# Transposed input kept for two blocks, a shorter ring of second-level operands, and stores issued by GpSimd, in a two-level Strassen-Winograd MLP kernel

## The chip, the cores and the metric

The kernel runs on one core of one Trainium2 chip. The metric is the device time in microseconds. Three runs of the kernel before took 933.02, 934.6 and 937.8 us; their median is 934.6 us. One more run was profiled.

## The reference

A batch of 16 x 512 = 8192 rows goes through two matrix products with a bias and a GELU between them:

```python
batch, m, k, h, n = 16, 512, 768, 3072, 768
y = np.matmul(x, w1) + b1
y = 0.5 * y * (1.0 + erf(y / np.sqrt(2.0)))
return np.matmul(y, w2).astype(np.float32)
```

All arrays are float32; the kernel computes its products in fp16 operands and adds in float32.

## The kernel before

The 8192 rows are taken in eight blocks of 1024 rows, numbered 0 to 7 (`sb` in the code). Each block goes through a first product (x with w1, then bias and GELU) and a second product (with w2).

Both products use Strassen's method in Winograd's form: a product of 2 x 2 blocks is made of seven smaller products of sums and differences of the blocks instead of eight. The seven are done in the order p1, p7, p5, p3, p6, p4, p2, each accumulated in a PSUM bank (`bX`, `bY`, `bW`, `bZ`), with copies and additions by ScalarE and VectorE between them.

- **First product** (`Unit1`, matmuls at L333): 12 units per block, one for each pair of 128 columns of the hidden layer. One of the seven products is three matmuls of 128 x 512; it takes 0.65 us. The weights of a unit, a tile `wt` of seven slots (672 KB), sit in a pool of four buffers. From block 2 on they are read from a scratch array `w1s` in DRAM, where block 1 has written them with their sums and differences (`load_wt`, L157; `keep`, L174). Unit k loads the weights of unit k + 3 in its slot 5.
- **Second product, blocks 0 and 1** (`Unit2`, L371): four units of seven products of twelve matmuls of 128 x 384; one product takes 1.95 us. Its operands lie in the array `w2o` in SBUF. The two halves of the output row block are kept in `osb`, of which there is one, and stored by SyncE (L385, L390). Beside it, `split_w2` makes the second-level operands of w2 in 28 steps: a subtraction by VectorE into a staging buffer (`stage`), then one or two writes of 288 KB to the scratch array `w2s` by SyncE (L206).
- **Second product, blocks 2 to 7** (`Unit3`, L422): a second level of the same method. Seven units of seven products of twelve matmuls of 128 x 192; one product takes 0.99 us. Each of the 49 products reads one second-level operand, 288 KB, which SyncE loads from `w2s` into a ring of 15 buffers (`load_ring`, L239): the load for product n + 15 is issued when product n is done. Results collect in four float32 arrays `par`; two additions by GpSimd (L467) finish one of them, and eight stores of 384 KB per block are issued by SyncE (L446).

x is loaded 128 rows at a time by GpSimd, with a cast to fp16, into one of three buffers `xh` (`load_x`, L248), and transposed by a DMA that SyncE issues (`transpose_dma`, L255) into `XT`. Block 0 alone transposes with TensorE. VectorE then makes four sums of the quarters of `XT` (`x_sums`); one of them is written over a quarter of `XT`. There is one `XT`: the eight loads and eight transposes for the next block are issued during the second product, once the last unit of the first product has read it.

The order of all work is written out by hand. `period(i, j, fill)` interleaves the seven products of unit i with the rest of unit j before it, and calls `fill` at six slots; `fill_mm1`, `fill_mm2_one` and `fill_mm2_two` issue there what belongs to the slots: loads, transposes, VectorE sums from the lists `soon`, `queue` and `slow`. Every engine works through its own queue in order: a DMA that waits holds all that stands behind it in SyncE's or GpSimd's queue.

Everything but the weights and x shares one SBUF array, `arena`, cut by hand. The staging buffers and the sums `GS` of blocks 0 and 1 lie over parts that blocks 2 to 7 use otherwise, and the first product's `tmps` lie over `par[0]` and `par[3]`.

## Time and profile before

| | |
|---|---|
| median of three runs | 934.6 us |
| the profiled execution's own time | 931.55 us |
| its span on the core | 929.7 us |
| TensorE busy | 869.7 us, 94% |
| VectorE busy | 665.6 us, 72% |
| ScalarE busy | 417.1 us, 45% |
| GpSimd busy | 116.4 us, 13% |
| DMA, mean over the span | 240 GB/s |
| granted TensorE clock, mean | 0.977 |

In the profile PE is TensorE, DVE is VectorE, ACT is ScalarE, POOL is GpSimd, and SPq is SyncE's DMA issue. A timeline row gives start in us, duration in us, engine, line and operation, out<-in, shape and count, and in brackets the idle time before it with its releaser. A row of waits gives the total in us, how often, and the longest. A row of a table of windows gives the window, its length, the busy time (and count of instructions) of PE, PE's weight loads, DVE, ACT and POOL, the granted clock, the DMA engines' busy share and GB/s. A row of DMA issues ends with KB and the us from issue to landing. Numbers after tile names are buffers (`bX_143`, `w1s_72`).

Block 2's first product runs from about 260 to 311 us of the span, its second to about 361. The blocks after it begin their first products at about 366, 478, 590, 704 and 815 us; block 7's second product ends the span.

### The profile page before, as it was taken

How to read it: one execution, taken by the hardware profiler on the slowest of the kernel's cores; microseconds unless marked ns; L12 is line 12 of the kernel's file. 1: busy time of each engine (PE TensorE's matmuls, PEld its weight loads, DVE VectorE, ACT ScalarE, POOL GpSimd, SP SyncE). 2: the span in 40 equal slices, each digit the busy share in tenths (PEclk: the TensorE clock that was granted, in tenths of full speed). 3: DMA queues.
4: the chain of work that ended last, by engine and by line, in shares of the span. 5: the costliest groups of instructions: out<-in, count | busy, mean ns of one | idle time of the engine just before them, and what ended most of it. 6: DMA issues, size and time to landing. Idle time of an engine off the chain costs nothing.

```text
span 929.7 us, 16276 instructions
## 1 busy us (share of the span) xinstructions
PE 869.7 (94%) x6276; PEld 565.6 (61%) x6276; DVE 665.6 (72%) x1151; ACT 417.1 (45%) x680; POOL 116.4 (13%) x146
## 2 busy tenths in 40 slices
PE   5999999997999997999989999799997999899997
PEld 2434654444544796447964499544994459854697
DVE  3688666663546896479965799467994679945997
ACT  2655117740167521774217732377213772157610
POOL 5552102300100012000210002000030000200002
PEclk7999999999999998999999999999998999999999
DMA  9998999959848599685997689965998749978485
GB/s 156 111 187 112 259 339 227 244 192 302 186 146 281 156 266 347 235 285 139 296 348 256 215 201 300 353 234 178 248 282 313 250 165 271 317 262 280 162 286 205
DMA packets 184206, 222.97 MB, mean 240 GB/s; under 512 B 106944, under 2 KB 127424, under 8 KB 184128
## 3 DMA queue, kind: packets, MB, share of 16 engines
q1 hardware_dynamic: 124736, 195.18, 65.1%
q0 software_dynamic: 59392, 26.75, 23.0%
q8 instruction: 49, 0.80, 0.3%
q14 instruction: 29, 0.24, 0.1%
HBM read 189.74 MB, written 47.87 MB: 256 GB/s over the span
## 4 chain that ended last, share of the span: by engine, by line
PE 66%; DMA 15%; DVE 12%; ACT 2%; issue 2%; POOL 1%; SPq 1%; DVEq 0%; ACTq 0%; POOLq 0%
PE bY_144 L333 9%; PE bY_145 L333 8%; PE bX_143 L333 6%; DVE arena L127 6%; PE bW L333 5%; PE bX_142 L333 5%; PE bZ L333 5%; DMA wt<-in_w_dram 4%; DMA wt<-w1s_72 4%; PE bY_145 L422 4%; PE bY_144 L422 4%; PE bW L422 3%; PE bZ L422 3%; PE bX_142 L422 2%; PE bX_143 L422 2%
## 5 line engine op out<-in xcount | busy, mean ns | idle before, releaser
L333 PEld LDWEIGHTS <-wt 128*128 128x128 f16 x2016 | 197.7, 99 | 271.4 <-DMA wt<-w1s_72 22.9
L422 PEld LDWEIGHTS <-arena 128*128 128x128 f16 x2664 | 226.0, 99 | 21.1 <-issue 16.6
L348 ACT ACTIVATE G_134<-arena,b1t 128x1024 f16<-128x1024 f32 x96 | 110.3, 1149 | 63.8 <-DVE arena L505 63.8
L127 DVE TENSOR_TENSOR arena<-arena 128x1536 f16<-128x1536 f16 (+5 forms) x176 | 127.7, 746 | 0.9
L492 ACT COPY pw<-bW 128x512 f32<-128x512 f32 (+1 forms) x146 | 80.9, 554 | 93.8 <-PE bW L422 44.3
L248 POOL DMA_DIRECT2D xh<-in_x_dram x56 | 29.9, 536 | 598.2 <-DMA XT<-xh 591.5
L482 DVE TENSOR_TENSOR arena<-bY_145,pw 128x512 f32<-128x512 f32 (+1 forms) x52 | 35.4, 681 | 94.9 <-PE bY_145 L333 69.0
L333 PE MATMUL bX_143<-XT,wt 128*128 128x512 f16 x288 | 80.1, 388 | 13.1 <-DMA wt<-w1s_72 12.9
L333 PE MATMUL bX_142<-XT,wt 128*128 128x512 f16 x288 | 80.5, 389 | 8.8 <-DMA wt<-w1s_72 8.8
L505 DVE TENSOR_TENSOR arena<-bZ,pw 128x512 f32<-128x512 f32 (+1 forms) x104 | 70.5, 678 | 19.6 <-PE bZ L333 13.8
L333 PE MATMUL bW<-XS_136,wt 128*128 128x512 f16 x288 | 80.4, 389 | 4.0 <-DVE wt L127 4.0
L333 PE MATMUL bY_144<-XT,wt 128*128 128x512 f16 x288 | 78.0, 379 | 3.5 <-DVE bZ L520 3.4
L482 DVE TENSOR_TENSOR arena<-bY_144,pw 128x512 f32<-128x512 f32 (+1 forms) x52 | 35.4, 681 | 63.1 <-PE bY_144 L333 35.8
L333 PE MATMUL bY_145<-XT,wt 128*128 128x512 f16 x288 | 77.8, 379 | 2.1 <-DVE bZ L520 1.2
L333 PE MATMUL bZ<-XS_138,wt 128*128 128x512 f16 x288 | 77.8, 379 | 0.0
L475 ACT COPY bY_145<-bX_143 128x512 f32<-128x512 f32 (+1 forms) x73 | 39.9, 547 | 83.3 <-DVE arena L454 39.5
L475 ACT COPY bY_144<-bX_142 128x512 f32<-128x512 f32 (+1 forms) x73 | 40.4, 554 | 69.8 <-DVE arena L454 39.6
L422 PE MATMUL bY_144<-arena 128*128 128x192 f16 x612 | 61.7, 253 | 5.4 <-DVE bZ L515 5.4
L422 PE MATMUL bY_145<-arena 128*128 128x192 f16 x612 | 60.5, 250 | 5.4 <-DVE bZ L515 5.4
L371 PEld LDWEIGHTS <-arena 128*128 128x128 f16 x384 | 38.0, 99 | 32.3 <-issue 7.0
L127 DVE TENSOR_TENSOR arena<-arena,G_133 128x1024 f16<-128x1024 f16 (+4 forms) x86 | 48.5, 564 | 1.8
L161 POOL DMA_DIRECT2D wt<-in_w_dram x48 | 39.5, 831 | 79.8 <-DVE wt L127 35.3
(87 smaller groups left out, 1178.5 us busy)
## 6 DMA issues: line engine op xcount, KB each, us to landing
out_dram<-arena SPq DMA_DIRECT2D x64, 384.0 KB, 6.3
xh<-in_x_dram POOLq DMA_DIRECT2D x56, 192.0 KB, 6.6
wt<-in_w_dram POOLq DMA_DIRECT2D x48, 192.0 KB, 7.3
arena<-in_w_dram POOLq DMA_DIRECT2D x16, 288.0 KB, 9.0
wt<-w1s_72 SPq DMA_DIRECT2D x6, 672.0 KB, 9.1
wt<-w1s_78 SPq DMA_DIRECT2D x6, 672.0 KB, 10.3
wt<-w1s_73 SPq DMA_DIRECT2D x6, 672.0 KB, 8.8
wt<-w1s_79 SPq DMA_DIRECT2D x6, 672.0 KB, 5.1
```

The lines of the kernel that those rows point to most:

```text
L127: nc.vector.tensor_tensor(out=o, in0=a, in1=b, op=op)
L161: nc.gpsimd.dma_start(out=wt[:, 2 * half:2 * half + 2, :, :].rearrange("p a k c -> p (a k) c"), in_=w1r[:, :, c0:c0 + P])
L248: nc.gpsimd.dma_start(out=xh, in_=xr[:, sb * 8 + t, :])
L333: nc.tensor.matmul(out=dst[:, 0:RH], lhsT=self.wt[:, slot, c, :], rhs=a[:, c, :], start=first and c == 0, stop=c == self.C - 1, skip_group ...
L348: nc.scalar.activation(out=G2[:, hi, :, :], in_=self.tmp, func=GELU, bias=b1t[:, NH + hi:NH + hi + 1])
L371: nc.tensor.matmul(out=dst[:, 0:N2], lhsT=a, rhs=w2o[:, slot, :, c, :], start=first and c == 0, stop=c == self.C - 1, skip_group_check=True)
L422: nc.tensor.matmul(out=dst[:, t * N4:(t + 1) * N4], lhsT=a, rhs=w[:, c, :], start=first and c == 0 and t == 0, stop=c == NQ - 1, skip_grou ...
L475: nc.scalar.copy(out=bY[u.g % 2][:, 0:u.F], in_=bX[u.g % 2][:, 0:u.F])
L482: nc.vector.tensor_tensor(out=u.c22(), in0=bY[u.g % 2][:, 0:u.F], in1=w[:, 0:u.F], op=ADD)
L492: nc.scalar.copy(out=w[:, 0:u.F], in_=bW[:, 0:u.F])
L505: nc.vector.tensor_tensor(out=u.c12(), in0=bZ[:, 0:u.F], in1=w[:, 0:u.F], op=ADD)
```

## The change

Four things change together.

- There are two arrays `XT`, used in turn by even and odd blocks. In blocks 2 to 6 the eight x loads and eight transposes of the next block are issued in the first product (units 1 to 8 and 3 to 10, slot 3) instead of the second. The sums of x stay in the last unit of the second product. Block 0's and block 1's stay where they were.
- The ring has 10 buffers instead of 15, which frees the space for the second `XT`. It is filled in units 3 to 7 of the first product. `stage` has four buffers instead of five, in `par[0]` and `par[3]`, and `GS` moves too. Since `tmps` lie there, the three steps of `split_w2` in block 1's first product are gone; 12 of the 28 steps run in block 0's second product (before: 15) and 16 in block 1's (before: 10).
- The weights for units 0, 1 and 2 of the next block are loaded in units 0, 5 and 6 of the second product (slot 6), before in units 4, 5 and 6.
- The eight stores per block at L446 are issued by GpSimd, not by SyncE.

```diff
-    XT = wp.tile([P, 2, 2 * KQ, RH], F16, name="XT")
+    XTs = [wp.tile([P, 2, 2 * KQ, RH], F16, name=f"XT{k}") for k in range(2)]
...
-    RING = 15
+    RING = 10
...
-    stage = [cut(o, WB, "p (c n) -> p c n", c=NQ)
-             for o in (*range(14 * NH * N4, o_par - 4 * NH * P - WB + 1, WB),
-                       o_par + 2 * PAR, o_par + 2 * PAR + WB)]
+    stage = [cut(o_par + k * PAR + d * WB, WB, "p (c n) -> p c n", c=NQ)
+             for k in (0, 3) for d in range(2)]
...
-    GS = [cut(o_par - (4 - k) * NH * P, NH * P, "p (c r) -> p c r", c=NH) for k in range(4)]
+    GS = [cut(o + k * NH * P, NH * P, "p (c r) -> p c r", c=NH)
+          for o in (14 * NH * N4, o_par + 2 * PAR) for k in range(2)]
...
-        def transpose_dma(t):
-            nc.sync.dma_start_transpose(out=xT_of(t), in_=xhs[t])
+        def transpose_dma(sb, t):
+            nc.sync.dma_start_transpose(out=xT_of(sb, t), in_=xhs[t])
...
             def store(self, r):
...
-                nc.sync.dma_start(out=orr[:, s0:s0 + 2, right * N2:(right + 1) * N2],
+                nc.gpsimd.dma_start(out=orr[:, s0:s0 + 2, right * N2:(right + 1) * N2],
...
         def fill_mm1(sb, k, slot):
...
-            if sb == 1 and slot == 2 and k % 4 == 2:
-                slow.pop(0)[1]()
+            if slot == 3 and sb >= ONE and sb + 1 < nsb:
+                if 1 <= k < 9:
+                    load_x(sb + 1, k - 1)
+                if 3 <= k < 11:
+                    transpose_dma(sb + 1, k - 3)
...
         def fill_mm2_one(sb, k, slot):
...
-            if slow and slot > 1 and (k > 0 or sb > 0):
+            if slot > 1 and len(slow) > (16, 0)[sb]:
                 slow.pop(0)[1]()
...
         def fill_mm2_two(sb, k, slot):
...
             if sb + 1 < nsb:
-                if k == 0 and slot == 1:
-                    load_next_x(sb + 1, range(3))
-                if k == 1 and slot == 4:
-                    for t in range(3):
-                        transpose_dma(t)
-                    load_next_x(sb + 1, range(3, 6))
-                if k == 3 and slot == 1:
-                    for t in range(3, 6):
-                        transpose_dma(t)
-                    load_next_x(sb + 1, range(6, 8))
-                if k in (4, 5, 6) and slot == 6:
-                    load_wt((sb + 1) * NH + k - 4)
-                if k == 4 and slot == 4:
-                    for t in range(6, 8):
-                        transpose_dma(t)
+                if k in (0, 5, 6) and slot == 6:
+                    load_wt((sb + 1) * NH + max(k - 4, 0))
                 if k == 6 and slot == 1:
                     prep_wt((sb + 1) * NH)
-                    x_sums(queue)
+                    x_sums(sb + 1, queue)
```

How the queues change is seen at three places. The first is SyncE's queue at the end of block 2's second product. L255 is a transpose of x, L239 a ring load, L446 a store, L157 a load of first-product weights (`w1s_72` and `w1s_78` are those of units 0 and 1). Before:

```order
L255 DMA_TRANSPOSE XT<-xh 128x6x128 x2
L239 DMA arena<-w2s_99 128x1152
L446 DMA out_dram<-arena 128x2x384 x2
L239 DMA arena<-w2s_104 128x1152
L157 DMA wt<-w1s_72 128x2688
L239 DMA arena<-w2s_100 128x1152
L239 DMA arena<-w2s_101 128x1152
L446 DMA out_dram<-arena 128x2x384 x2
L157 DMA wt<-w1s_78 128x2688
L446 DMA out_dram<-arena 128x2x384 x2
L157 DMA wt<-w1s_73 128x2688
```

With the change, at the same place:

```order
L239 DMA arena<-w2s_99 128x1152
L239 DMA arena<-w2s_104 128x1152
L239 DMA arena<-w2s_100 128x1152
L239 DMA arena<-w2s_101 128x1152
L157 DMA wt<-w1s_78 128x2688
L157 DMA wt<-w1s_73 128x2688
L157 DMA wt<-w1s_79 128x2688
```

Transposes and stores have left, and the load of `w1s_72` has moved 35 rows ahead, to the fifth row of the second product. The second place is SyncE's queue in units 4 to 6 of block 2's first product, with the change:

```order
L157 DMA wt<-w1s_81 128x2688
L239 DMA arena<-w2s_88 128x1152
L239 DMA arena<-w2s_89 128x1152
L255 DMA_TRANSPOSE XT_136<-xh 128x6x128
L157 DMA wt<-w1s_76 128x2688
L239 DMA arena<-w2s_119 128x1152
L239 DMA arena<-w2s_90 128x1152
L255 DMA_TRANSPOSE XT_136<-xh 128x6x128
```

Before, the same rows stand there without the two transposes. The third place is SyncE's queue in block 1's second product, from the transposes of its third unit on (L206 is a write of a second-level operand, L386 and L391 are the output stores, which stood at L385 and L390). With the change:

```order
L255 DMA_TRANSPOSE XT_135<-xh 128x6x128 x3
L206 DMA w2s_131<-arena 128x1152
L206 DMA w2s_128<-arena 128x1152
L206 DMA w2s_129<-arena 128x1152
L386 DMA out_dram<-arena 128x768
L206 DMA w2s_111<-arena 128x1152
L206 DMA w2s_105<-arena 128x1152
L391 DMA out_dram<-arena 128x768
L206 DMA w2s_109<-arena 128x1152
L206 DMA w2s_106<-arena 128x1152
L255 DMA_TRANSPOSE XT_135<-xh 128x6x128 x2
```

Before, no write of a second-level operand was left here: the three transposes were followed by the two output stores and the two transposes.

42 lines of the change are left out of this document (21 added, 21 removed).

## The prediction

> **What bounds the kernel now.** I read part 1 of the page first, then TensorE's waits, then the timeline around them.
>
> ```profile
> span 929.7 us, 16276 instructions
> PE 869.7 (94%) x6276; PEld 565.6 (61%) x6276; DVE 665.6 (72%) x1151; ACT 417.1 (45%) x680; POOL 116.4 (13%) x146
> ```
>
> ```profile
> PE bX_143 L333 <- DMA wt<-w1s_72: 12.9, 3, 5.3
> PE bX_142 L333 <- DMA wt<-w1s_72: 8.8, 2, 5.9
> ```
>
> TensorE is busy for 94%, so only its 60 us of idle time, and what follows each idle stretch, can be won. The largest wait (in total us, times, longest) is 12.9 + 8.8 = 21.7 us in five places: the first weights of a block, at the five turns from the second product of blocks 2 to 6 into the next block's first product. Every other row of that view is smaller. The timeline of TensorE shows each turn: the product before the wait, the wait, and the first product after which the pace is again one per 0.65 us (L333) or 0.99 us (L422).
>
> ```profile
> 359.98 1.15 PE L422 MATMUL bX_142<-arena 128*128 128x192 f16 x12
> 366.40 1.46 PE L333 MATMUL bX_143<-XT,wt 128*128 128x512 f16 x3 [5.27 <-DMA wt<-w1s_72]
> 373.73 0.81 PE L333 MATMUL bX_143<-XT,wt 128*128 128x512 f16 x3
> ...
> 473.77 1.15 PE L422 MATMUL bX_143<-arena 128*128 128x192 f16 x12
> 477.84 1.46 PE L333 MATMUL bX_142<-XT,wt 128*128 128x512 f16 x3 [2.91 <-DMA wt<-w1s_72]
> 484.08 0.81 PE L333 MATMUL bX_142<-XT,wt 128*128 128x512 f16 x3
> ...
> 583.97 1.15 PE L422 MATMUL bX_142<-arena 128*128 128x192 f16 x12
> 596.54 0.81 PE L333 MATMUL bX_143<-XT,wt 128*128 128x512 f16 x3
> ...
> 696.57 1.15 PE L422 MATMUL bX_143<-arena 128*128 128x192 f16 x12
> 711.31 0.81 PE L333 MATMUL bX_142<-XT,wt 128*128 128x512 f16 x3
> ...
> 810.87 1.15 PE L422 MATMUL bX_142<-arena 128*128 128x192 f16 x12
> 814.65 1.08 PE L333 MATMUL bX_143<-XT,wt 128*128 128x512 f16 x3 [2.63 <-DMA wt<-w1s_72]
> 821.24 0.81 PE L333 MATMUL bX_143<-XT,wt 128*128 128x512 f16 x3
> ```
>
> Between the first and last row of each turn stand four products of the second kind and three of the first: 4 x 0.99 + 3 x 0.65 = 5.9 us of work. The elapsed times are 13.75, 10.31, 12.57, 14.74 and 10.37 us; the losses are 7.8, 4.4, 6.7, 8.8 and 4.5, together **32.2 us**. So a turn costs half as much again as its wait. The rest is the clock, here in the stretch right after the shortest of the waits (the last three columns are granted clock, DMA share, GB/s):
>
> ```profile
> 814.65:818.00 3.35, 3.35 (x17) 2.45 (x18) 0.31 (x1) 0.57 (x1) 0.00 (x0) 0.57 1.04 409
> ```
>
> The clock is at 0.57 for some 3 us even after a wait of 2.63 us. The Trainium skill ("TensorE: Matmul & The Clock Gate", Part 1) puts the drop to half rate after an idle window of about 3.4 us; by that rule the two turns with waits of 2.91 and 2.63 us would lose only these, and the sum below would be smaller by (4.4 - 2.9) + (4.5 - 2.6) = 3.4 us. The row decides against it here.
>
> **Why the weights are late.** SyncE's timeline before the first turn:
>
> ```profile
> 335.20 7.53 SPq L255 DMA_TRANSPOSE XT<-xh  x3
> ...
> 354.29 1.41 SPq L446 DMA_DIRECT2D out_dram<-arena  x2
> ...
> 356.34 0.47 SPq L157 DMA_DIRECT2D wt<-w1s_72  x1
> ```
>
> SyncE issues in order. The weight load goes out at 356.34, behind eight transposes (three of them in the first row) and the stores, and lands at 366.4, 10 us later, since the DMA engines are full (second row below; the columns are as above):
>
> ```profile
> 260.00:311.00 51.00, 51.00 (x239) 23.20 (x238) 31.90 (x54) 38.71 (x61) 0.00 (x0) 1.00 0.60 207
> 311.00:365.00 54.00, 48.21 (x562) 46.31 (x560) 50.48 (x85) 12.94 (x25) 9.09 (x10) 1.00 1.00 264
> ...
> 872.00:925.00 53.00, 51.09 (x597) 49.23 (x596) 49.13 (x85) 12.46 (x25) 4.79 (x2) 1.00 0.73 235
> ```
>
> These are block 2's first and second product and block 7's second. Block 7 has no successor, so no x and no transposes: that is the second product as the change leaves it.
>
> **The change part by part.** *First weights (L157), transposes and x moved out of the second product.* The program issues the load in unit 0 instead of unit 4 of seven units of 7 us, some 40 us before its use. The sums of x stay in unit 6:
>
> ```profile
> 358.48 0.96 DVE L127 TENSOR_TENSOR XS_136<-XT 128x1536 f16<-128x1536 f16 x1 [0.20 <-DMA XT<-xh]
> ...
> 362.49 0.95 DVE L127 TENSOR_TENSOR XS_138<-XT,XS_137 128x1536 f16<-128x1536 f16 x1
> ```
>
> With no wait, the new block's first product would start at 361.0, the one that reads XS_136 at 362.6 (0.65 + 0.99 later) and the one that reads XS_138 at about 368.5; the sums ended at 359.4 and 363.4, so 3 us of cover stay. Gain: 32.2 us if nothing else is late there.
>
> *Ring of 10.* A load is issued when the product ten ahead has been read, so it has 9 products, 9 x 0.99 = 8.9 us. Block 7's second product has nothing but ring loads and stores about; its slowest ring load:
>
> ```profile
> arena<-w2s_93 SPq DMA_DIRECT2D x1, 288.0 KB, 4.8
> ```
>
> (us from issue to landing): 4 us of cover. Cost 0. In block 2's full stretch the slowest early one took longer than the 8.9 us, and there each late load would cost TensorE some 0.4 us, more where a clock drop follows:
>
> ```profile
> arena<-w2s_92 SPq DMA_DIRECT2D x1, 288.0 KB, 9.3
> ```
>
> *x and transposes in the first product.* Here is the price. Its weights and ring loads now:
>
> ```profile
> 378.46 0.34 SPq L157 DMA_DIRECT2D wt<-w1s_74  x1
> ```
>
> ```profile
> 387.98 0.81 PE L333 MATMUL bX_143<-XT,wt 128*128 128x512 f16 x3
> ```
>
> ```profile
> wt<-w1s_74 SPq DMA_DIRECT2D x1, 672.0 KB, 3.8
> ```
>
> ```profile
> DMA packets 3452, 10.35 MB, mean 211 GB/s; under 512 B 384, under 2 KB 384, under 8 KB 3448
> ```
>
> A unit takes 7 products x 0.65 = 4.53 us. The weights issued at 378.46 are read at 387.98, 9.5 us later, and land after 3.8: slack 5.7 us. The last row is block 2's first product (262 to 311): 10.35 MB in about 30 us of DMA time (0.60 x 49 to 51) is 345 GB/s, so 2.0 us for a weight tile, 0.85 for a ring load: 3.7 us per unit with two ring loads. What an x load and a transpose cost together no row isolates. Base: the two second products differ by 54 x 1.00 - 53 x 0.73 = 15.3 us; block 2's has two weight tiles more (4.0) and two stores less (2 x 1.14 us at 345 GB/s), so 13.6 us for eight pairs, **1.7 us** each. Upper end: three transposes held SyncE for 7.53 us, 2.5 each, and 384 KB of x at 345 GB/s take 1.1: 3.6 us. In units 3 to 7 pairs and ring loads coincide. Base: 3.7 + 1.7 = 5.4 us per unit, 0.9 over, 4.4 us behind after five units, inside the slack: no stall. Upper end: 7.3, 2.8 over, 13.9 behind, 8.2 us of stall per block, 41 us over blocks 2 to 6. Below nothing it cannot go. I take 0.6 us per block, **3 us**, near the base, because that comes from whole stretches while SyncE's 7.53 us also holds queueing behind ring loads.
>
> *Stores from GpSimd.* They leave SyncE's order; GpSimd has only two additions per block beside them, and the buffers they free are wanted tens of us later. Only the last store is on the path, after the last addition:
>
> ```profile
> 925.44 0.56 DVE L454 TENSOR_TENSOR arena<-bY_145,arena 128x384 f32<-128x384 f32 x1 [0.43 <-PE bY_145 L422]
> ```
>
> ```profile
> 343.93 0.53 POOL L248 DMA_DIRECT2D xh<-in_x_dram  x1 [13.37 <-DMA XT<-xh]
> ```
>
> From the addition's end to the span's end are 3.7 us. GpSimd's issue of one x load (128 rows) takes 0.53 us against SyncE's 0.34 for a weight load; a store has 256 rows. Plus 0.2 us if only the issue differs, up to 3 us if the landing nearly doubles: I take **1 us**.
>
> *Blocks 0 and 1.* w2's split keeps 16 of its 28 steps for block 1's second product (10 before) and has none in block 1's first product. Now:
>
> ```profile
> 135.15 2.12 PE L371 MATMUL bZ<-arena 128*128 128x384 f16 x12 [0.48 <-DVE arena L127]
> ...
> 191.09 0.81 PE L333 MATMUL bY_144<-XT,wt 128*128 128x512 f16 x3 [1.56 <-DVE bZ L520]
> ...
> 224.29 2.11 PE L371 MATMUL bZ<-arena 128*128 128x384 f16 x12
> 231.50 3.73 PE L371 MATMUL bY_144<-arena 128*128 128x384 f16 x12 [5.09 <-ACT bY_144 L475]
> 235.06 2.11 PE L371 MATMUL bY_145<-arena,G_134 128*128 128x384 f16 x12
> ```
>
> ```profile
> 189.66 0.32 SPq L206 DMA_DIRECT2D w2s_123<-arena  x1
> ```
>
> The wait of 1.56 us on VectorE's copy ended 1.4 us after the write of a split step was issued, in a queue of additions that VectorE works through in order; I count it as gone. The other stall, 235.06 - 224.29 less two products of 1.95, 6.9 us, is an output store stuck behind transposes, weights and writes of w2; all of these stay, with one write more in front (0.85 us), and units 2 and 3 get transposes and writes together, as block 0 has them, where the first row (0.48 us) is the only wait. Plus 1.5, bounds 0 and another 6.9. Net **0**.
>
> *Sum:* -32.2 + 3 + 1 + 0 = -28.2 us; the span goes from 929.7 to 901.5. The profiled run's own time is 931.55, 1.85 over its span, and the median of the runs shown, 934.6, is 3 us above that: **906 us**.
>
> **The rivals.** *Half given back:* a pair costs 2.5 us, between the bounds: 6.2 per unit, 1.7 over, 8.4 behind, 2.7 of stall per block, 13 us; 934.6 - 32.2 + 13 + 1 = 916. For it: a transpose alone is at 2.5 in the 7.53 us row. Against: the 15.3 us difference.
>
> *The wait moves, no gain:* at the turn the second-level operands or the sums of x arrive late instead, as the ring is a third shorter. For it: the 9.3 us above. Against: block 7's 4.8 at most. A loss like the present one gives 932.
>
> *Slower, the first product becomes the DMA's:* the weights of units 6 to 11 come late, in each of five blocks, with a clock drop behind each. Price at the upper end: -32.2 + 41 + 1 = +10, 944. It decides from 6.5 us of stall per block, which is a pair at 3.3 us. Against: block 2's first product has 0.60 of DMA time used; eight pairs at 1.7 add 13.6 us and take five ring loads (4.3 us) away, 40 of 51 us. The Trainium skill ("DMA: Bandwidth & Descriptors", Issuing engines are not separate DMA queues) says that all issuers share the same 16 engines; by it GpSimd's x is no cheaper than SyncE's would be, which is how this rival counts it.
>
> **How the numbers follow.** Forecast 0.66 (900 to 911), half given back 0.16 (911 to 926), no gain 0.07, slower 0.11. Range 898 to 926: the low end is the whole 32.2 gained with the runs' own spread of 3 us, the high end the second case's. The likeliest case's own range is 900 to 911. A change of 0.5% (4.7 us) is about what can be told from none: faster 0.82, same 0.07, slower 0.11.
>
> **What would show it.** Right: the five waits on w1s_72 gone, no clock under 0.95 around the turns; DMA share near 0.75 in second and 0.85 in first products; weights landing after 4 to 9 us in units 3 to 8; ring loads under 6 us. Wrong: L333 waiting for weights or L422 for ring loads late in a product; a landing of weights above 9.5 us; block 1 losing more than one store's wait.

## The result, and the profile after

The changed kernel takes 906.86 us (median of four runs, 906.44 to 908.34), the kernel before, in four runs beside it, 933.81 us. The ratio is 0.9711 with a 95% interval of 0.9673 to 0.9748: 27 us, or 2.9%, faster. The prediction said 906. Its sum came out, but several of its terms did not, and one edit was priced without its main effect, as the experiments show; that the errors nearly cancel is luck.

The head of the page after, to be read against the first two rows of the prediction (the profiled execution's own time is 908.34 us):

```profile
span 906.2 us, 16269 instructions
PE 860.2 (95%) x6276; PEld 560.6 (62%) x6276; DVE 666.9 (74%) x1151; ACT 417.5 (46%) x680; POOL 148.1 (16%) x194
```

TensorE's busy time fell by 9.5 us although it executes the same 6276 matmuls: the stretches at a lowered clock at the turns are gone, which is likely most of it. GpSimd's rose by 32 us; it now issues 48 stores.

TensorE's waits after (total us, times, longest). Lines past the first sixty or so stand one lower than before: L333 is now L334, L422 is L423, L515 is L516; in experiments whose edit adds lines they move by one or a few more.

```profile
PE bY L423 <- DVE bZ L516: 13.3, 12, 1.8
...
PE bX L334 <- DMA wt<-w1s: 1.5, 3, 0.8
```

The 21.7 us of waits on the first weights are gone; of all waits on loads from `w1s` 1.5 us are left, in three places inside first products. The largest wait is now one that the prediction did not name: VectorE's addition that writes `bZ` (L516; the last expectation below calls it a copy), 13.3 us where the two rows of before give 5.4 + 5.4 = 10.8.

The first turn in TensorE's timeline, which answers to the prediction's first pair of rows:

```profile
363.03 1.15 PE L423 MATMUL bX<-arena 128*128 128x192 f16 x12
364.02 0.81 PE L334 MATMUL bX<-XT,wt 128*128 128x512 f16 x3
364.67 1.15 PE L423 MATMUL bY<-arena 128*128 128x192 f16 x12
...
368.94 1.46 PE L334 MATMUL bX<-XT,wt 128*128 128x512 f16 x6
```

From the first row to the last are 5.91 us, exactly the work of four products of 0.99 and three of 0.65 us; before it was 13.75. The other four turns take 5.9 us as well.

The granted clock and the DMA share by stage, with the columns of before (the last three are clock, DMA share and GB/s): block 2's first product, its second, and block 3's first product.

```profile
262.00:313.00 51.00, 49.91 (x231) 22.07 (x229) 31.23 (x53) 37.96 (x60) 2.64 (x5) 1.00 0.87 225
313.00:367.00 54.00, 51.66 (x592) 48.94 (x591) 51.76 (x87) 14.60 (x28) 8.61 (x8) 1.00 0.87 291
...
366.00:413.00 47.00, 46.95 (x234) 22.30 (x232) 28.27 (x47) 34.72 (x55) 6.12 (x11) 1.00 1.04 271
```

The clock is at 1.00 throughout. The DMA share fell in the second product, to 0.87 where the prediction expected some 0.75, and rose in the first further than the 0.85 expected: 0.87 in block 2, and 1.04 in the part of block 3's that the last row covers. Yet TensorE hardly waits for it, because the loads have room. The loads issued in block 3's first product (366 to 413 us; the last number is the median from issue to landing):

```profile
wt<-w1s SPq DMA_DIRECT2D x8, 672.0 KB, 6.3
arena<-w2s SPq DMA_DIRECT2D x10, 288.0 KB, 7.6
```

Weights land after 6.3 us in the middle, inside the 9.5 that they have. The slowest of these eight takes 10.0 us and the slowest in block 2 10.1; the 1.5 us of waits lie in these two blocks.

**Where the time went, by stretches.** One profile of a kernel cannot be compared with one of another over the whole span: block 1's first product differs by up to 5 us between profiles of kernels whose code there is the same (shown below). So I cut the span at three places of TensorE's timeline: the first L334 of block 1, the first L372 of block 1's second product, and the first L334 of block 2 (131.25, 196.71 and 253.66 us in the profile after).

| profile | block 1, first product | block 1, second | block 2 to the end |
|---|---|---|---|
| before | 64.4 | 56.9 | 677.1 |
| after | 65.5 | 57.0 | 652.5 |
| after, second profile | 60.4 | 57.9 | 652.7 |

From block 2 on the change gains 24.5 us, and two profiles of it agree within 0.2 us. The parts: the five turns -32.2; the longer of a block's two waits for the addition into `bZ` grows from 1.33 to 1.75 us in each of six blocks, +2.5; the end after the last addition grows from 3.7 to 7.3 us, +3.6; block 2's first product takes 59.9 instead of 58.3 us, +1.6. Their sum is -24.5. (In the second profile block 2's first product takes 58.6 us, and about as much is lost in later first products instead.)

### The profile page after: what moved, and what is told of

It reads as the page before. It is cut to its first block, busy times and chain, and to the rows that moved or that the text cites. A ratio compares the mean times of both kernels' runs of the same rounds, so it can differ in the third digit from the quotient of the medians.

```text
span 906.2 us, 16269 instructions
## 1 busy us (share of the span) xinstructions
PE 860.2 (95%) x6276; PEld 560.6 (62%) x6276; DVE 666.9 (74%) x1151; ACT 417.5 (46%) x680; POOL 148.1 (16%) x194
## 4 chain that ended last, share of the span: by engine, by line
PE 67%; DVE 14%; DMA 10%; issue 4%; POOL 2%; ACT 2%; SPq 0%; POOLq 0%; DVEq 0%; ACTq 0%
PE bY L334 17%; PE bX L334 11%; PE bY L423 8%; DVE arena L127 7%; PE bW L334 5%; PE bZ L334 5%; PE bY L372 5%; PE bX L423 5%; DMA wt<-in_w_dram 4%; DMA wt<-w1s 4%; PE bX L372 3%; PE bW L423 3%; PE bZ L423 3%; DMA out_dram<-arena 1%; PE bZ L372 1%
## 5 line engine op out<-in xcount | busy, mean ns | idle before, releaser
L334 PEld LDWEIGHTS <-wt 128*128 128x128 f16 x2016 | 197.1, 98 | 250.9 <-issue 19.6
L423 PEld LDWEIGHTS <-arena 128*128 128x128 f16 x2664 | 221.2, 98 | 20.8 <-issue 15.1
L483 DVE TENSOR_TENSOR arena<-bY,pw 128x512 f32<-128x512 f32 (+1 forms) x104 | 70.8, 680 | 153.9 <-PE bY L334 98.7
L334 PE MATMUL bY<-XT,wt 128*128 128x512 f16 x576 | 155.8, 379 | 7.5 <-DVE bZ L521 7.3
L334 PE MATMUL bX<-XT,wt 128*128 128x512 f16 x576 | 143.0, 381 | 1.6 <-DMA wt<-w1s 1.5
L476 ACT COPY bY<-bX 128x512 f32<-128x512 f32 (+1 forms) x146 | 80.4, 551 | 131.9 <-DVE arena L455 105.0
L349 ACT ACTIVATE G<-arena,b1t 128x1024 f16<-128x1024 f32 x96 | 110.3, 1149 | 64.3 <-DVE arena L506 64.3
L423 PE MATMUL bY<-arena 128*128 128x192 f16 x1224 | 115.6, 246 | 13.3 <-DVE bZ L516 13.3
L334 PE MATMUL bW<-XS,wt 128*128 128x512 f16 x288 | 78.7, 383 | 4.0 <-DVE wt L127 4.0
L334 PE MATMUL bY<-XS,wt 128*128 128x512 f16 x288 | 79.1, 384 | 1.0 <-DVE wt L127 0.4
L334 PE MATMUL bZ<-XS,wt 128*128 128x512 f16 x288 | 78.5, 382 | 0.0
L423 PEld LDWEIGHTS <-G 128*128 128x128 f16 x864 | 72.5, 98 | 4.8 <-issue 1.9
L372 PEld LDWEIGHTS <-arena 128*128 128x128 f16 x384 | 38.1, 99 | 31.5 <-issue 7.0
## 6 DMA issues: line engine op xcount, KB each, us to landing
wt<-w1s SPq DMA_DIRECT2D x72, 672.0 KB, 6.7
w1s<-wt SPq DMA_DIRECT2D x12, 672.0 KB, 4.4
```

Of the source, the lines that this page charges most:

```text
L334: nc.tensor.matmul(out=dst[:, 0:RH], lhsT=self.wt[:, slot, c, :], rhs=a[:, c, :], start=first and c == 0, stop=c == self.C - 1, skip_group ...
L349: nc.scalar.activation(out=G2[:, hi, :, :], in_=self.tmp, func=GELU, bias=b1t[:, NH + hi:NH + hi + 1])
L372: nc.tensor.matmul(out=dst[:, 0:N2], lhsT=a, rhs=w2o[:, slot, :, c, :], start=first and c == 0, stop=c == self.C - 1, skip_group_check=True)
L423: nc.tensor.matmul(out=dst[:, t * N4:(t + 1) * N4], lhsT=a, rhs=w[:, c, :], start=first and c == 0 and t == 0, stop=c == NQ - 1, skip_grou ...
L476: nc.scalar.copy(out=bY[u.g % 2][:, 0:u.F], in_=bX[u.g % 2][:, 0:u.F])
L483: nc.vector.tensor_tensor(out=u.c22(), in0=bY[u.g % 2][:, 0:u.F], in1=w[:, 0:u.F], op=ADD)
```

## The experiments

The times are medians; a ratio is to the kernel before, run beside the experiment, with its 95% interval; "from block 2 on" is the stretch of the table, where the kernel after has 652.5 and 652.7.

**1. The stores back on SyncE.** All else as after the change.

```diff
-                nc.gpsimd.dma_start(out=orr[...],
+                nc.sync.dma_start(out=orr[...],
```

> The changed kernel with one part undone: the eight stores per block are issued by SyncE again. Theory (the stores' move to GpSimd gave nothing to the turns and costs time at the end and beside the additions): the five turns stay without a wait for weights, the span's tail after the last addition goes back from 7.3 to about 3.7 us, the wait for L516 in each of six blocks from 1.75 to about 1.33 us; together about 6 us less, 901 us. Rival (a store that waits for VectorE in SyncE's queue holds the weights of units 1 and 2 and the last ring loads): waits for weights return at the turns, 2 to 6 us each with the clock drop, 910 to 930 us.

Measured: 921.25 us (919.25 to 924.7), ratio 0.9874 (0.9834 to 0.9914); 672.0 us from block 2 on, 19.4 more than after the change. TensorE's waits in this kernel:

```profile
PE bW L423 <- DMA arena<-w2s: 6.9, 6, 1.7
PE bZ L423 <- DMA arena<-w2s: 6.5, 4, 2.3
...
PE bY L423 <- DMA arena<-w2s: 2.6, 2, 2.2
```

The rival's size was right, my theory's was not, and what comes late are the ring loads, not the weights: no wait for weights returns, and the five turns still take 5.9 us each. The theory's other two parts came out (the wait for L516 is back at 10.8 us in all, the end after the last addition at 3.6), so the ring loads cost some 25 us, of which these parts hide 6. SyncE's timeline (start, us, instruction, count) and the largest reason of its waiting stores show why:

```profile
335.44 6.26 SPq L239 DMA_DIRECT2D arena<-w2s  x7
346.45 2.87 SPq L447 DMA_DIRECT2D out_dram<-arena  x2
349.42 3.64 SPq L239 DMA_DIRECT2D arena<-w2s  x7
```

```profile
SPq L447 <- POOL arena L468: 39.9, 12, 4.7
```

A store in SyncE's queue waits for GpSimd's addition, up to 4.7 us, and the ring loads behind it are not issued until then: seven of them go out in 3.64 us from 349.42 on, where one per 0.99 us is the pace. In this kernel's last block eight ring loads stand 4.3 to 7.4 us between the release of their buffer (the end of the last matmul that reads it) and their issue, where a load that is not held has 10.2 us from release to use, and then land after 3.6 to 8.4. The kernel before has such holds too: in its last block three loads stand 6.2 to 7.1 us behind stores, but with 15 buffers they have 15.2 us to use, and nothing waits. With the stores on GpSimd every one of the last nine loads is issued 0.03 us after its release. So the stores' move is what makes the short ring free.

**2. Only block 7's stores back on SyncE.**

```diff
-                nc.gpsimd.dma_start(out=orr[...],
+                eng = nc.sync if self.sb == nsb - 1 else nc.gpsimd
+                eng.dma_start(out=orr[...],
```

> The changed kernel with only block 7's stores issued by SyncE. Theory (the tail is the landing of stores issued by GpSimd): the tail after the last addition goes from 7.3 to about 3.7 us and the wait for L516 in block 7 from 1.72 to 1.33; about 4 us less, 903 us. Rival (the tail is the DMA engines' and not the issuer's): no change, 906 to 908 us.

Measured: 902.07 us (901.7 to 902.65), ratio 0.9665 (0.9634 to 0.9697). The median and the end (3.6 us after the last addition; experiment 11 shows why) are as expected, but the median owes part of it to scatter: from block 2 on it takes 650.2 us, only 2.4 less, and 1.2 of these lie in block 2's first product, which the edit does not touch (58.7 us; the kernel after itself took 59.9 and 58.6). The gain of about 4 us at the end is partly taken back by the same hold as in experiment 1, ring loads behind block 7's other stores; the view of TensorE's waits has

```profile
PE bY L423 <- DMA arena<-w2s: 2.3, 2, 1.9
```

**3. The kernel before with the early weight load alone.**

```diff
-                if k in (4, 5, 6) and slot == 6:
-                    load_wt((sb + 1) * NH + k - 4)
+                if k in (0, 5, 6) and slot == 6:
+                    load_wt((sb + 1) * NH + max(k - 4, 0))
```

> The kernel before with one part of the change alone: the weights of units 0, 1 and 2 are loaded in units 0, 5 and 6 of the second product; x, transposes and stores stay where they were. Theory (order and full DMA engines both count): the wait for w1s_72 is gone, but w1s_78 is issued where it was, behind transposes and stores, and lands about 10 us later, 3 to 5 us after unit 1 wants it, so that the turns lose about 3 us each instead of 6.4; 915 to 922 us. Rival A (the order of one load is all): 32 us less, 902 us. Rival B (the DMA engines' time is all, whatever is ordered first): 930 to 935 us.

Measured: 925.66 us (919.27 to 931.26, ten runs), ratio 0.9926 (0.9888 to 0.9965); 670.2 us from block 2 on. Of the 32.2 us of the turns only some 7 are won, and the time lies between the theory's range and rival B's. The weights of unit 1 do come late, as the theory has it (issued at 361.7 us, landed at 372.6), but it left out the ring loads. The wait goes to whatever comes next in the same full stretch:

```profile
PE bX L422 <- DMA arena<-w2s: 9.5, 7, 3.3
PE bX L333 <- DMA wt<-w1s: 8.6, 5, 3.1
...
PE bY L422 <- DMA arena<-w2s: 5.3, 5, 2.1
```

**4. The kernel after with the weights issued late again.** The reverse: transposes, x and stores stay moved.

```diff
-                if k in (0, 5, 6) and slot == 6:
-                    load_wt((sb + 1) * NH + max(k - 4, 0))
+                if k in (4, 5, 6) and slot == 6:
+                    load_wt((sb + 1) * NH + k - 4)
```

> The kernel after the change, with the next block's first weights issued in unit 4 again, as before the change, instead of unit 0. It tells what of the turn's 32.2 us is due to the earlier issue and what to the transposes, x loads and stores that left the second product. My theory: without them the load lands in about 6 us, over 10 us before its use; from the start of block 2 to the end the time stays within 1 us of the changed kernel's 652.5. Rival: the load competes with ring loads and stores at the end of the product, and the turns wait again for 1 to 3 us each: 5 to 15 us more.

Measured: 905.95 us (903.66 to 906.68), ratio 0.9724 (0.9691 to 0.9756); 652.1 us from block 2 on. My theory holds: the early issue of the weights is worth nothing once the second product is clear of the other transfers. The 32.2 us are due to those. Of the three, x and the transposes are what counts for the weights: in experiment 1 the stores are back on SyncE, though with the early issue, and each turn still takes 5.9 us. No run moves x and the transposes alone.

**5. The kernel before with its stores on GpSimd alone.**

```diff
-                nc.sync.dma_start(out=orr[...],
+                nc.gpsimd.dma_start(out=orr[...],
```

> The kernel before with one part of the change alone: the stores at L446 are issued by GpSimd. Theory (a store costs SyncE 0.4 to 0.7 us of issue, and the weights stand behind two of them, but the DMA engines stay full): the weights go out 1 to 2 us earlier per turn, 5 to 10 us less, against 3.6 us at the end and about 2.5 us beside the additions: 927 to 935 us. Rival (stores that wait for VectorE were what held the weights): the turns lose 10 us less or better, 915 to 922 us.

Measured: 946.59 us (943.38 to 947.3), ratio 1.0135 (1.0098 to 1.0172); 689.9 us from block 2 on, 12.8 more than before. Both theories missed: the edit alone costs. TensorE's waits and the turn into block 3:

```profile
PE bX L422 <- DMA arena<-w2s: 25.2, 7, 6.6
```

```profile
365.86 1.44 PE L422 MATMUL bX<-arena 128*128 128x192 f16 x8 [6.64 <-DMA arena<-w2s]
```

In four of the five turns a last ring load of the block is now late, by 5.0 to 6.6 us. The load that TensorE waits for in the row above, and its counterpart in the kernel before (us from issue to landing):

```profile
arena<-w2s SPq DMA_DIRECT2D x1, 288.0 KB, 11.0
```

```profile
arena<-w2s_99 SPq DMA_DIRECT2D x1, 288.0 KB, 6.0
```

It lands 5.0 us more slowly: GpSimd issues four stores from 348.8 to 355.7 us, ahead of this load and beside it, where in the kernel before the first two stores go out right behind it, at 354.29. And it is issued later: two transposes ahead of it hold SyncE for 4.89 us, where before they held it for 3.33.

```profile
349.87 4.89 SPq L255 DMA_TRANSPOSE XT<-xh  x2
```

That the stores are the reason for the slower landing is argued from this order, not shown by a run of its own.

The same edit is worth +13 us before the other edits and -19 us after them. The Trainium skill ("DMA: Bandwidth & Descriptors", Issuing engines are not separate DMA queues) says that issuing from several engines saves only the issuing time, "which is usually small relative to the DMA itself". The issuing alone is small here too, 0.73 us for a store. What the page does not count is the wait: a DMA that waits for a result holds all that stand behind it, which is the row of 39.9 us in experiment 1.

**6. Without x loads and transposes in the first products of blocks 2 to 6.**

```diff
-            if slot == 3 and sb >= ONE and sb + 1 < nsb:
+            if slot == 3 and sb >= ONE and sb + 1 < nsb and False:
```

> The kernel after the change, but without the x loads and the transposes in the first products of blocks 2 to 6: blocks 3 to 7 compute with the x that lies there already, so part of the computation is left out (the loading of five blocks' x). It measures what the x loads and transposes cost in the first products, which the prediction put at 0.6 us a block, 3 us in all, between 0 and 41. My theory: the trace after the change has 1.5 us of waits for weights in three places in the first products, so taking the transfers away gives back 1 to 4 us: 903 to 906. Rival (half given back): the price is 2.7 us a block and hides in gaps that the table of waits does not name: 890 to 896. Third: the transfers' price is nothing and the time is 906 to 908.

Measured: 900.95 us (900.09 to 901.05), ratio 0.964 (0.9591 to 0.969). That is 6 us less than after and looks like twice the prediction's price, but by stretches most of it lies elsewhere. Block 1's first product, which the edit does not touch, took 60.7 us in this profile; from block 2 on are 648.9 us, 3.6 less, of which 1.7 lie behind the last addition. The stretch from block 2's start to TensorE's last wait for `bZ`, in block 7, is 635.6 us in the profile after (253.66 to 889.22), 635.7 in the second one, and 633.6 here: the x loads and transposes cost **2.0 us**, against 3 forecast. The 1.7 us at the end are not the last store's: it lands 3.1 us after its issue in both kernels. They are GpSimd's closing instruction, a DRAIN behind its last store, which takes 6.30 us after the change and 4.58 here (first the kernel after, then this one; the third number is the longest, in ns). Why it is shorter here no run shows.

```profile
L778 POOLq DRAIN  x3: 46/93/6302, 899.2 to 906.0; - x3
```

```profile
L778 POOLq DRAIN  x3: 46/93/4583, 893.8 to 898.9; - x3
```

The landings in block 3's first product, from the same window as above:

```profile
wt<-w1s SPq DMA_DIRECT2D x8, 672.0 KB, 4.0
arena<-w2s SPq DMA_DIRECT2D x10, 288.0 KB, 4.6
```

So the pairs of an x load and a transpose delay the middle weight tile by 2.3 us and the middle ring load by 3.0, and nearly all of this stays inside the slack.

What a pair costs the DMA engines can be read here too. Block 3's whole first product, first after the change and then here (the last two columns are DMA share and GB/s):

```profile
363.99:420.33 56.34, 55.81 (x283) 26.75 (x281) 35.97 (x62) 40.18 (x62) 6.49 (x11) 1.00 0.98 260
```

```profile
358.98:414.88 55.90, 55.73 (x282) 26.74 (x280) 36.20 (x61) 40.38 (x62) 2.18 (x3) 1.00 0.58 204
```

That is 0.98 x 56.34 = 55 us of DMA time against 0.58 x 55.90 = 32, 23 us for eight pairs. Over blocks 2 to 6 it is 260 against 157 us, or **2.6 us a pair**, in both profiles after: not the 1.7 us of the prediction's base but the 2.5 of its rival "half given back". The price in DMA time was the rival's; the price in TensorE's time was not.

**7. Seven ring buffers instead of ten.**

```diff
-            return ring[((sb - ONE) * 49 + n) % RING]
+            return ring[((sb - ONE) * 49 + n) % LEAD]     # LEAD = 7
...
-                load_ring(self.sb, n + RING)
+                load_ring(self.sb, n + LEAD)
...
-                    for m in range(2 * (k - 3), min(2 * (k - 2), RING)):
+                    for m in range(2 * (k - 3), min(2 * (k - 2), LEAD)):
```

> The kernel after the change with 7 of the 10 ring buffers in use, so that a load has 6 products, 5.9 us, from issue to use instead of 8.9. It measures how far the ring of 10 is from its edge. After the change the ring loads of a second product (block 3) land after 3.5 to 4.7 us, one after 5.5, but the first ten of each block are loaded in the first product, where they have more time. My theory: 5.9 us still cover nearly all, so at most a late load or two per block of under 1 us each: 907 to 913. Rival: the ring of 10 is at its edge, as the prediction's rival of a wait that moves to the ring would have it; each load is then some 1 to 3 us late and the product runs at the pace of the loads: 920 or more.

Measured: 908.81 us (907.63 to 913.27), ratio 0.9735 (0.9679 to 0.9791); 657.0 us from block 2 on, 4.3 more than after. The rows of the ring in TensorE's waits:

```profile
PE bY L424 <- DMA arena<-w2s: 3.3, 4, 1.3
...
PE bX L424 <- DMA arena<-w2s: 1.1, 2, 0.9
```

With one more of 0.2 us these are seven late loads in six blocks, 4.6 us in all, the longest somewhat above the theory's 1 us: with 5.9 us of lead the ring is just past its edge, with 8.9 it has some room. With the stores gone from SyncE the ring of 10 is not what limits.

**8. Both additions of GpSimd ahead of both stores.** After the change GpSimd adds, issues a store, adds, issues a store.

```diff
                     for r in range(2):
                         nc.gpsimd.tensor_tensor(out=self.dst[:, r], ..., op=ADD)
+                    for r in range(2):
                         self.store(r)
```

> The kernel after the change with GpSimd's two additions at the end of a block ahead of both stores, where now it adds, issues a store (0.75 us), adds, issues a store. My theory: the issue between the additions pushes the second one back, and VectorE's operation beside it, which ends 0.82 us after that addition in both traces, with it; the wait of TensorE for that operation, 1.75 us in the middle after the change and 1.33 before it, goes back to 1.33 in six turns: 904 to 905.5. Rival: the wait is set by the order of VectorE's own work, and nothing moves: 906.5 to 907.5.

Measured: 903.23 us (900.95 to 905.86), ratio 0.9668 (0.9614 to 0.9721); 649.4 us from block 2 on, 3.2 less. The wait is back at its size of before, -2.5 us:

```profile
PE bY L423 <- DVE bZ L517: 10.8, 12, 1.3
```

In the timelines of GpSimd and VectorE of the kernel after, the second addition stands behind the store, and VectorE's addition beside it takes 2.52 us where the same kind takes 0.94 alone (the first of VectorE's rows runs beside GpSimd's first addition, 456.84 to 459.23, and is not slowed):

```profile
460.31 1.82 POOL L468 TENSOR_TENSOR arena<-arena 128x768 f32<-128x768 f32 x1
```

```profile
457.48 0.55 DVE L455 TENSOR_TENSOR arena<-bX,arena 128x384 f32<-128x384 f32 x1
...
460.44 2.52 DVE L127 TENSOR_TENSOR arena<-arena 128x1536 f16<-128x1536 f16 x1
...
463.35 0.94 DVE L127 TENSOR_TENSOR arena<-arena 128x1536 f16<-128x1536 f16 x1
```

GpSimd ends at 462.13, VectorE 0.83 us later, at 462.96: read with the 0.94 us, it stood still until GpSimd had finished and then did its work. In all fourteen profiles, wherever such an addition of VectorE (both inputs in SBUF) starts beside one of GpSimd's, it ends 0.81 to 0.83 us behind it; VectorE's additions with one input in a PSUM bank (L455, L481) keep their 0.55 us. The 0.75 us of store issue between GpSimd's additions delay both: from the start of its first to the end of its second are 5.29 us after the change and 4.89 in this experiment, the 0.4 us by which TensorE's wait differs.

**9. Block 1's weight loads for block 2 moved behind its second units.** On top of experiment 2.

```diff
-                for n in range(4):
+                for n in range(4 if sb == 0 else 0):
+                    load_wt((sb + 1) * NH + n)
+            if sb == 1 and (k, slot) in ((2, 6), (3, 1)):
+                for n in ((0, 1) if k == 2 else (2, 3)):
                     load_wt((sb + 1) * NH + n)
```

> The kernel after the change, with block 7's stores issued by SyncE (902.07 alone) and block 1's four weight loads for block 2 moved behind its second units (two in unit 2's last slot, two in unit 3's second), instead of in one burst with three x loads and three transposes in unit 1. My theory: the store of the output at 219.14 us lands 12 us later because these loads stand ahead of it in the same DMA engines; without them TensorE's stall of 6.9 us in block 1's second product goes, while the first weights are still there in time for block 2: 895 to 897. Rival: the transposes and the writes of w2 alone hold the store, and the stall shrinks by 2 us at most, or block 2's first weights come late and take it back: 900 to 903.

Measured: 905.96 us (905.33 to 908.11), ratio 0.9694 (0.9634 to 0.9753), 4 us slower than the kernel it starts from. The stall of 5 us in block 1's second product did go: that stretch took 52.9 us instead of 57.9. But it came back a few products later. The loads of weights go out right ahead of the next two stores of the output (SyncE's timeline), ScalarE waits 12.4 us until it may write `osb` again, and TensorE for ScalarE:

```profile
241.35 2.16 SPq L157 DMA_DIRECT2D wt<-w1s  x4
...
244.09 0.37 SPq L386 DMA_DIRECT2D out_dram<-arena  x1
```

```profile
256.01 0.48 ACT L389 COPY arena<-bX 128x384 f32<-128x384 f32 x1 [12.39 <-DMA out_dram<-arena]
```

```profile
246.30 0.82 PE L334 MATMUL bX<-XT,wt 128*128 128x512 f16 x3 [1.24 <-DMA wt<-w1s]
...
257.03 1.44 PE L334 MATMUL bY<-XS,wt 128*128 128x512 f16 x3 [5.36 <-ACT bY L477]
```

From block 2 on it takes 659.8 us, 9.6 more than experiment 2. The time lies outside the theory's range and the rival's, and block 2's first weights come 1.24 us late as the rival has it. My theory's mechanism held and its gain did not: there is one `osb`, it is stored several times, and whichever store follows the burst is held.

**10. The changed kernel again.**

> The changed kernel once more, unedited. In the profiles so far, block 1's first product (from its first L334 to the first L372 of its second product) took between 60.4 and 65.5 us, in kernels whose code up to there is the same; in the profile of the changed kernel it took 65.5. My theory: this stretch, where the DMA engines are loaded beyond a share of 1.0, varies from execution to execution, so a profile of the same kernel can show 60.4 to 65.5 there, everything after block 2's start stays at 652 to 653 us, and the median lies between 902 and 908. Rival: the 65.5 belongs to the changed kernel's instructions, and it shows again: 906 to 908.

Measured: 905.11 us (902.15 to 910.33), ratio 0.9724 (0.9682 to 0.9766). Block 1's first product took 60.4 us here and 65.5 in the first profile of the same kernel: the scatter is between executions. VectorE's wait for the last raw weights of the stretch, in the profile before, the first one after, and this one:

```profile
187.82 1.15 DVE L127 TENSOR_TENSOR wt<-wt 128x384 f16<-128x384 f16 x3 [1.49 <-DMA wt<-in_w_dram]
```

```profile
187.89 1.14 DVE L127 TENSOR_TENSOR wt<-wt 128x384 f16<-128x384 f16 x3 [3.98 <-DMA wt<-in_w_dram]
```

```profile
183.83 1.14 DVE L127 TENSOR_TENSOR wt<-wt 128x384 f16<-128x384 f16 x3 [0.17 <-DMA wt<-in_w_dram]
```

In the first profile after TensorE then waits 3.25 us for VectorE, and the clock is at 0.50 for 3.4 us behind that wait; in the second it does not wait. The load's landing makes the difference, and the DMA share does not tell the two apart: from 150 to 190 us it is 1.24 before, 1.25 in the first profile after and 1.27 in the second. (A share above 1 means that packet times overlap, so they cannot be added up as if they came one after another.) Over all profiles, the three kernels with the old code of this stretch took 63.0 to 64.4 us there, the eleven with the new one 60.4 to 65.5 with nine of them below 62.4, middle 61.4. Some 2 us of gain from the three writes of w2 that the change takes out of this stretch is likely; three profiles on one side do not prove it.

**11. The additions first, and only the last product's stores on SyncE.** The parts of experiments 2 and 8 that pay, together.

```diff
-                nc.gpsimd.dma_start(out=orr[...],
+                eng = nc.sync if self.sb == nsb - 1 and self.i > 5 else nc.gpsimd
+                eng.dma_start(out=orr[...],
...
+                    for r in range(2):
                         self.store(r)
```

> The kernel after the change with GpSimd's two additions ahead of both stores, and the stores of block 7's last product alone on SyncE (with all of block 7's on it, TensorE waited 1.95 us for the last ring load). My theory, from block 2's start to the end against the changed kernel's 652.5: -2.5 from the additions, as measured alone, and -3 from a landing of the last store in 3.7 us instead of 7.3: 646 to 648, a time of 897 to 902 according to block 1. Rival: the last store lands late on either queue, and only the 2.5 show: 649.5 to 650.5.

Measured: **899.95 us** (897.69 to 900.86), ratio 0.9659 (0.9632 to 0.9687), the best kernel here; 646.25 us from block 2 on, as expected. The ends of the span, first after the change (span 906.2 us), then here (span 897.4 us): VectorE's last addition, the last two stores with the us to their landing, and GpSimd's DRAIN here, to be read against the one in experiment 6:

```profile
898.33 0.56 DVE L455 TENSOR_TENSOR arena<-bY,arena 128x384 f32<-128x384 f32 x1 [0.43 <-PE bY L423]
```

```profile
out_dram<-arena POOLq DMA_DIRECT2D x2, 384.0 KB, 3.0
```

```profile
893.22 0.56 DVE L456 TENSOR_TENSOR arena<-bY,arena 128x384 f32<-128x384 f32 x1 [0.43 <-PE bY L423]
```

```profile
out_dram<-arena SPq DMA_DIRECT2D x2, 384.0 KB, 2.5
```

```profile
L780 POOLq DRAIN  x3: 46/93/6140, 890.1 to 897.1; - x3
```

From the addition's end to the end of the span are 7.3 us with GpSimd's store and 3.6 us with SyncE's. The expected gain came, but not for the expected reason: GpSimd's last store lands only some 0.6 us more slowly and is issued 0.3 us later. The rest is the DRAIN. After the change it starts with the last store, at 899.2, and ends at 905.5, 3.2 us after that store has landed (902.3), and the program's end waits for it. Here GpSimd's last store is an earlier one, so its DRAIN starts at 890.1 and is over at 896.2, before SyncE's last store lands at 896.4.

**12. Product 5's additions put off by a unit.** On top of experiment 11: the additions and stores that end product 5 (`finish5`) run in unit 5, slot 4.

```diff
                 if self.p == 5:
-                    for r in range(2):
-                        tt(par[1][:, r], par[1][:, r], self.dst[:, r], ADD)
...
+                    put_off.append(self)
...
+            if k == 5 and slot == 4:
+                put_off.pop(0).finish5()
```

> As the kernel with the additions first and the last product's stores on SyncE, but product 5's additions on VectorE and GpSimd are put off to unit 5, slot 4, some 9 us later. My theory: the waits of TensorE for VectorE's copy (L517, 1.33 us in each of six blocks) come from VectorE standing still beside GpSimd's additions while it is busiest; later, where it works on little, they shrink to below 0.5: another 5 us less, 641 to 643 from block 2's start to the end, a time of 892 to 897. Rival: VectorE is held up just the same at the new place and the wait moves there, or the stores that now come 9 us later delay the next block's first product: 646 to 652.

Measured: 905.66 us (905.02 to 906.23), ratio 0.9724 (0.9699 to 0.9749); 654.5 us from block 2 on, 8.3 more than experiment 11. The rival holds, and the time from block 2 on is beyond even its range. VectorE is stopped at the new place just the same, the last of three additions that take 4.30 us together beside GpSimd's two, and TensorE waits there instead:

```profile
885.12 4.30 DVE L127 TENSOR_TENSOR arena<-arena 128x768 f32<-128x768 f32 x3
```

```profile
PE bY L423 <- ACT bY L481: 6.8, 6, 1.1
PE bY L423 <- DVE bZ L521: 5.6, 11, 0.6
```

These two rows are 12.4 us, against 10.8 in experiment 11. The stores follow later and in one burst,

```profile
891.04 4.35 POOL L448 DMA_DIRECT2D out_dram<-arena  x6
```

and by stretches most of the 8.3 us lie where they then land: the first products of blocks 3 to 7 take 0.7 to 1.4 us longer each, 4.7 together, and the end after the last addition 3.0 (6.6 instead of 3.6): SyncE's last store lands after 5.0 us, and GpSimd's DRAIN ends 0.8 us later still.

## Why the prediction came out, step by step

- *Five turns, -32.2:* right. Each turn takes the 5.9 us of its work, the clock stays at 1.00. But the step gave the credit to three edits together; experiments 3 and 4 separate them. What pays is that the other transfers leave the second product; the early issue of the weights, alone worth 7 us, is worth nothing beside that.
- *Ring of 10, cost 0:* the cost is right, the reason incomplete. The step compared 8.9 us of lead with 4.8 us from issue to landing and found 4 us of cover, but the lead starts when the buffer comes free, and a load may stand in SyncE's queue before it is issued. With the stores in that queue it stands up to 7.4 us, and the cover is gone (experiment 1).
- *Stores from GpSimd, +1:* this is where the prediction was wrong. It priced the edit at the tail alone. Inside the program the edit is what the ring of 10 rests on, 19 us from block 2 on. It also cost more than priced: the tail grew by 3.6 us, above the upper bound of 3, and for another reason than the landing that the step had in mind, which is 0.6 us slower; 2.7 us are GpSimd's DRAIN at the program's end, which the step did not have (experiment 11). And the issue between the two additions added 2.5 us to the waits for VectorE, which the step did not see, because it said of GpSimd that it "has only two additions per block beside them" and not who waits for those.
- *x and transposes, +3:* measured 2.0, but the working failed. A pair takes 2.6 us of DMA time, not 1.7 (experiment 6). By the step's own arithmetic that is 3.7 + 2.6 = 6.3 us in a unit of 4.53, 8.9 us behind after five units, 3.2 of stall in each of five blocks and 16 us in all. In the first profile the weights came at most 6.2 us later than the 3.9 that they take without the pairs, against 5.7 us of slack, so TensorE waited for 1.5 us. So slack covers the transfers, as the step said, but adding up DMA times as if they came one after another overstates the delay; why it is smaller no run shows. Too low a price and too much delay for it cancelled: that is luck. The step's own signs said so: weights above 9.5 us (10.1) and L333 waiting for weights, both named as signs of being wrong, and ring loads above 6 us (7.6 in the middle of block 3's first product).
- *Blocks 0 and 1, net 0:* about -1.5 (-2.3 in block 1's first product, +0.8 in its second, both between the middle values of three profiles with the old code and of ten or eleven with the new), with a reason that was wrong. The wait of 1.56 us was put down to a write of w2; VectorE, which TensorE waited for, had itself waited for a load of raw weights (the first row of experiment 10), and the same wait is 3.25 us in one profile of the changed kernel and absent in another.

Together: -32.2 + 2.0 + 3.6 + 2.5 - 1.5 = -25.6, where the medians give -27. The 906 is right partly by luck: the +5 that it missed at the tail and the additions stood against over-estimates elsewhere (1 us for the pairs, 1.5 in blocks 0 and 1) and inside the few us by which block 1 scatters. The three rivals fell by their times: no half of the gain was given back, although a pair has the price in DMA time at which that rival starts; no wait moved to the turn; the first product, with a DMA share of up to 0.98 over its whole length, did not become the DMA's.

## What to carry to other kernels

An edit that is priced at nothing because another covers it should be priced without that other one too: here the stores' engine, thought a detail, carried the shorter ring. For a load in an in-order queue, count the time from when it could go, including all waits of what stands ahead of it, not from issue to landing. A transfer's time on the DMA engines is not yet a delay: ask which load it makes late, and by how much more than that load's slack. And before comparing profiles by their spans, cut them at fixed places of the program: a stretch that no edit touches may scatter by more than the effect that is sought.

## What the runs showed of the hardware that I had not expected

- An addition of VectorE with both inputs in SBUF stands still for as long as GpSimd's addition beside it runs and ends 0.81 to 0.83 us after it; one with an input in a PSUM bank runs on at its 0.55 us (experiment 8). The Trainium skill ("SBUF — State Buffer", Who interferes with whom) describes the port pair that the two share as an exclusive lock and not a split of bandwidth; the trace agrees.
- At the end of the program GpSimd executes a DRAIN. In six profiles whose last store GpSimd issues it ends 6.3 us after the start of that store and 3.2 us after its landing; in the seventh, without x loads, 4.6 and 1.4 us. The store itself lands after 3.1 us from GpSimd and 2.5 from SyncE, so most of the 3.6 us that the end loses, 2.7, lies in the DRAIN (experiments 6 and 11).
- The same kernel took 60.4 and 65.5 us in a stretch with a DMA share of some 1.25, and within 0.2 us the same time in the 652 us behind it.
